# Down-projection steps between pairs of the up-projection, weight sums by accumulating loads, embedding projection moved

## Chip, core and metric

The kernel runs on one core of one Trainium2 chip. The metric is the device time of one launch in microseconds (us). The times shown are a median of three runs, and one further execution of the same program was profiled.

## What is computed

One decoder layer over 512 tokens of width 1024, in float32. The change lies in the last third, the gated MLP and the embedding behind it:

```python
h = rms_norm(x, ffn_norm[i])
act, lin = jnp.split(h @ w_ffn_up[i], 2, axis=-1)
act = causal_dwconv(act, w_ffn_conv[i]) + b_ffn_conv[i]
x = x + (jax.nn.gelu(act) * lin) @ w_ffn_down[i]
g = jax.nn.sigmoid(rms_norm(x, ple_norm[i]) @ w_ple_gate[i])
x = x + g * (p[i] @ w_ple_proj[i])
return rms_norm(x, final_norm)
```

The hidden width is 2816, 22 blocks of 128.

## The kernel before

Every float32 product is made of three matmuls on fp32r halves: a weight tile `raw` is loaded, ScalarE rounds it to `whi` (L164) and VectorE subtracts to get `wlo` (L165, the function `wsplit`); `raw` has four buffers in this part, `whi` and `wlo` four each, so a tile is split at most four split tiles ahead of its use. A step's weights are two split tiles, a pair's are four.

The up-projection goes in 11 pairs, `up(j)`: four products of 24 matmuls (two blocks of the gate half, two of the linear half), into the four PSUM banks of `mm_ps`. What follows each product (convolution, gelu, product of the halves) is done on ScalarE and VectorE; then `combine` (L277 to L286) makes from the pair's tile `g` the seven token-side factors of a Strassen-Winograd product, `ch` and `cl`. There is one buffer of these for four pairs.

The down-projection is three such products, `down(0)` to `down(2)`, over four, four and three pairs; `strassen` runs the seven steps. A step multiplies one factor by one block of the weights or by a sum of blocks, 24 matmuls (18 in down 2), and adds its result from PSUM to `x2` on VectorE (L1080). The blocks are loaded by SP, and the sums T1 to T4 are made in place by GpSimd or VectorE (L304). Down 0 runs after pair 4, down 1 after pair 10, down 2 straight behind it. In down 2, the additions are followed by the next norm (square on ScalarE, mean and power on GpSimd, L377 and L384; scaling on VectorE, L387), by the transposes x3n0T to x3n3T on TensorE (L410) and by copies to `h3h` and `h3l` (L412, L413).

Behind all that, p is loaded, transposed (pT, L1123) and multiplied by `w_ple_proj` (tiles pb from pTh); then comes the gate's product from `h3h`, and the end. A scheduler sets the order on each engine from the program order and from the priorities that `with ahead()` gives; each engine then works in that order.

Of the kernel before, what the change touches and what calls it, by code (L numbers as in the profile page):

```python
# [43 lines left out]
def tile_hybrid_block(  # L44
# [226 lines left out]

    WINO = ((0, "11"), (3, "T1"), (4, "T2"), (6, "22"), (1, "21"), (5, "T3"), (2, "T4"))

    def combine(g2, ch, cl, j):
# [3 lines left out]
        G.tensor_tensor(tmp[:, 0, :], a21, a22, op=ALU.add)  # L280
        G.tensor_tensor(tmp[:, 2, :], a1[:, 0, :], a21, op=ALU.subtract)
        G.tensor_tensor(tmp[:, 1, :], tmp[:, 0, :], a1[:, 0, :], op=ALU.subtract)
        G.tensor_tensor(tmp[:, 3, :], a1[:, 1, :], tmp[:, 1, :], op=ALU.subtract)
        for c, src in ((slice(0, 2), a1), (2, a22), (slice(3, 7), tmp)):
            S.copy(ch[:, c, j, :], src)
            V.tensor_tensor(cl[:, c, j, :], src, f32(ch[:, c, j, :]), op=ALU.subtract)  # L286

    def strassen(src, ch, cl, kh, add):
# [8 lines left out]
        pieces = [slice(k, min(k + 2, kh)) for k in range(0, kh, 2)]

        def sums(dst, x, y, eng):

            for q in pieces:
                eng.tensor_tensor(r[y][:, q, :], r[x][:, q, :], r[y][:, q, :], op=ALU.subtract)  # L304
# [4 lines left out]

        X = [mm_ps(f"sx{uid()}") for _ in range(2)]  # L310
        Z, Y = [], []
        for c, n in WINO:
            with ahead():
                if n == "11":
                    load(1, 1)
                    load(1, 2)
                    load(2, 2)
                elif n == "T1":
                    sums("T1", "12", "11", G)
                elif n == "T2":  # L320
                    sums("T2", "22", "T1", V)
                elif n == "21":
                    load(2, 1)
                elif n == "T3":

                    sums("T3", "22", "12", V)
                elif n == "T4":
                    sums("T4", "21", "T2", G)
                ws = split(n)
            if n == "T1":  # L330
                Z = [mm_ps(f"sz{uid()}") for _ in range(2)]
            elif n == "21":
                Y = [mm_ps(f"sy{uid()}") for _ in range(2)]
            ps = Z if n in ("T1", "22") else Y if n == "21" else X
            for t in range(2):
                tok = slice(t * P, (t + 1) * P)
                for k in range(kh):
                    hi, lo = ws[k // 2]
                    a, b = ch[:, c, k, tok], cl[:, c, k, tok]
                    first, last = k == 0 and n in ("11", "T1", "21"), k == kh - 1  # L340

                    TE.matmul(ps[t], lhsT=a, rhs=hi[:, k % 2, :], start=first, stop=False, skip_group_check=True)
                    TE.matmul(ps[t], lhsT=a, rhs=lo[:, k % 2, :], start=False, stop=False, skip_group_check=True)
                    TE.matmul(ps[t], lhsT=b, rhs=hi[:, k % 2, :], start=False, stop=last, skip_group_check=True)
                th, h = {"11": (0, 0), "T1": (2, 1), "T2": (0, 1), "22": (0, 1), "21": (0, 0), "T3": (2, 1), "T4": (2, 0)}[n]
# [769 lines left out]
    pt = [piece(f"pt{i}").rearrange("p (t d) -> p t d", t=2) for i in range(2)]  # L1115
    with ahead():
        for i in range(2):
            nc.sync.dma_start(pt[i], p[256 * i : 256 * i + 256, :].rearrange("(t q) d -> q t d", q=P))
    pT = []
    for k in range(2):  # L1120
        ps = sm_ps(f"pT{k}")
        for t in range(NT):
            TE.transpose(ps[:, t * P : (t + 1) * P], pt[t // 2][:, t % 2, k * P : (k + 1) * P], ident)  # L1123
        pT.append((piece(f"pTh{k}", R), piece(f"pTl{k}", R)))
        S.copy(pT[k][0], ps)
        V.tensor_tensor(pT[k][1], ps, f32(pT[k][0]), op=ALU.subtract)

    pj = [[piece(f"pj{t}_{h}") for h in range(2)] for t in range(NT)]
    for h in range(2):
        cols = slice(h * 512, (h + 1) * 512)  # L1130
        proj_b(w_ple_proj[:, cols], pT, 2, lambda t, ps: S.copy(pj[t][h], ps))
# [85 lines left out]
```

## Time and profile before

| | us |
|---|---|
| median of three runs | 1198.25 (1194.9 to 1203.29) |
| the profiled execution, its own time | 1203.02 |
| its span in the trace | 1201.2 |
| TensorE busy in it | 1164.5 |

The rows further down are of the profiled execution; its span starts at 0. PE is TensorE's matmul, DVE VectorE, ACT ScalarE, POOL GpSimd, SP the engine that issues most loads. A matmul's duration overlaps the next one's; the pace is the distance of two starts. Stretches in rows are in us from the start of the span.

### The profile page before, as it was taken

To read this page: it belongs to the slowest core of one execution; us is meant where nothing else is said; L and a number is where in the kernel's file an instruction comes from. 1 tells how busy PE (TensorE), PEld (TensorE's weight loads), DVE (VectorE), ACT (ScalarE), POOL (GpSimd) and SP (SyncE) were. 2 spreads that over 40 slices of the span, in tenths; PEclk is the share of its full clock that TensorE was granted. 3 is DMA by queue.
4 is the path that set the end of the run, shared out by engine and by line. 5 is a ranking of instruction groups with operands and counts; after the bars stand their busy time and mean duration, and the time that the engine had idled before them with its cause. 6 is when DMAs were issued, how large, how long until landed. Compare 5 with 4: busy or idle time off the path is not lost. (4 is left out here: it accounts for less than half of the span.)

```text
span 1201.2 us, 14024 instructions
## 1 busy us (share of the span) xinstructions
PE 1164.5 (97%) x5540; PEld 961.9 (80%) x5540; DVE 692.6 (58%) x810; ACT 515.5 (43%) x828; POOL 213.3 (18%) x213
## 2 busy tenths in 40 slices
PE   6999999999999999999999999999999999998796
PEld 6887787888887678888888888988888888876685
DVE  5866647667557546343333343566686665589735
ACT  4566283572382226443333232354334343343543
POOL 7003104031013000000110110112230211233202
PEclk9998999999999999999999999999999999999899
DMA  7332122222322243224233223633225333121501
GB/s 205 106 105 71 35 71 71 70 76 66 106 71 70 70 141 105 70 71 105 71 88 104 76 101 97 166 106 105 71 70 161 85 105 105 36 79 59 178 1 71
DMA packets 145825, 108.75 MB, mean 91 GB/s; under 512 B 5328, under 2 KB 124752, under 8 KB 145760
## 3 DMA queue, kind: packets, MB, share of 16 engines
q1 hardware_dynamic: 145184, 105.76, 30.2%
q10 hardware_dynamic: 576, 2.10, 0.5%
q8 instruction: 44, 0.72, 0.2%
q14 instruction: 21, 0.17, 0.0%
HBM read 105.75 MB, written 2.10 MB: 90 GB/s over the span
## 5 line engine op out<-in xcount | busy, mean ns | idle before, releaser
L165 DVE TENSOR_TENSOR wlo<-raw,whi 128x1024 fp32r<-128x1024 f32 x208 | 277.6, 1340 | 267.1 <-ACT whi L164 266.7
L164 ACT CAST whi<-raw 128x1024 fp32r<-128x1024 f32 (+2 forms) x209 | 216.5, 1039 | 388.4 <-PE pa L170 223.8
L169 PE MATMUL pa<-h1h,whi 128*128 128x512 f32 (+1 forms) x416 | 160.8, 387 | 0.2 <-ACT h1h L412 0.2
L171 PE MATMUL pa<-h1h,wlo 128*128 128x512 f32 (+1 forms) x416 | 157.9, 380 | 0.0
L170 PE MATMUL pa<-h1l,whi 128*128 128x512 f32 (+1 forms) x416 | 157.2, 378 | 0.1
L169 PE MATMUL pa<-h2h,whi 128*128 128x512 f32 (+1 forms) x384 | 142.8, 372 | 0.0
L170 PE MATMUL pa<-h2l,whi 128*128 128x512 f32 (+1 forms) x384 | 142.8, 372 | 0.0
L171 PE MATMUL pa<-h2h,wlo 128*128 128x512 f32 (+1 forms) x384 | 142.6, 372 | 0.0
L249 PE MATMUL pb<-whi,h1h 128*128 128x512 f32 x256 | 99.9, 395 | 0.8 <-DVE accb L677 0.8
L250 PE MATMUL pb<-wlo,h1h 128*128 128x512 f32 x256 | 99.9, 390 | 0.0
L251 PE MATMUL pb<-whi,h1l 128*128 128x512 f32 x256 | 99.5, 392 | 0.0
L169 PEld LDWEIGHTS pa<-h1h,whi 128*128 128x128 f32 x416 | 79.8, 192 | 15.2 <-issue 1.2
L170 PEld LDWEIGHTS pa<-h1l,whi 128*128 128x128 f32 x416 | 79.7, 192 | 14.7 <-issue 1.0
L171 PEld LDWEIGHTS pa<-h1h,wlo 128*128 128x128 f32 x416 | 79.5, 191 | 13.9 <-issue 0.2
L170 PEld LDWEIGHTS pa<-h2l,whi 128*128 128x128 f32 x384 | 72.4, 189 | 12.5
L169 PEld LDWEIGHTS pa<-h2h,whi 128*128 128x128 f32 x384 | 72.4, 188 | 12.4
L171 PEld LDWEIGHTS pa<-h2h,wlo 128*128 128x128 f32 x384 | 72.4, 189 | 12.4
L249 PEld LDWEIGHTS pb<-whi,h1h 128*128 128x128 f32 x256 | 48.1, 188 | 10.5 <-DVE accb L677 1.2
L251 PEld LDWEIGHTS pb<-whi,h1l 128*128 128x128 f32 x256 | 48.1, 188 | 9.8
L250 PEld LDWEIGHTS pb<-wlo,h1h 128*128 128x128 f32 x256 | 48.1, 188 | 9.3
L542 DVE SCALAR_TENSOR_TENSOR acc<-pa,prm,acc 128x511 f32<-128x511 f32 (+2 forms) x72 | 52.6, 742 | 2.9 <-ACT acc L540 2.0
L170 PE MATMUL pa<-obl,whi 128*128 128x512 f32 x128 | 52.0, 406 | 0.0
(375 smaller groups left out, 2036.7 us busy)
## 6 DMA issues: line engine op xcount, KB each, us to landing
raw<-in_w_in_dram SPq DMA_DIRECT2D x48, 512.0 KB, 5.2
raw<-in_w_ffn_up_dram SPq DMA_DIRECT2D x44, 512.0 KB, 5.1
raw<-in_w_in_dram SPq DMA_DIRECT2D x16, 1024.0 KB, 5.0
raw<-in_w_branch_b_dram SPq DMA_DIRECT2D x32, 256.0 KB, 3.7
raw<-in_w_ffn_down_dram SPq DMA_DIRECT2D x8, 1024.0 KB, 5.2
raw<-in_w_branch_a_dram SPq DMA_DIRECT2D x8, 512.0 KB, 4.8
raw<-in_w_out_dram SPq DMA_DIRECT2D x4, 1024.0 KB, 5.2
raw<-in_w_ple_gate_dram SPq DMA_DIRECT2D x4, 1024.0 KB, 5.2
```

Source lines behind the costliest of these rows:

```text
L164: S.copy(hi, raw)
L165: eng.tensor_tensor(lo, raw, f32(hi), op=ALU.subtract)
L169: TE.matmul(ps, lhsT=lh, rhs=rh, start=first, stop=False)
L170: TE.matmul(ps, lhsT=lh, rhs=rl, start=False, stop=False)
L171: TE.matmul(ps, lhsT=ll, rhs=rh, start=False, stop=last)
L249: TE.matmul(pss[t], lhsT=a, rhs=hi[:, kk, :], start=first, stop=False)
L250: TE.matmul(pss[t], lhsT=a, rhs=lo[:, kk, :], start=False, stop=False)
L251: TE.matmul(pss[t], lhsT=b, rhs=hi[:, kk, :], start=False, stop=last)
L542: V.scalar_tensor_tensor(out=acc[:, s:], in0=ps[:, : T - s], scalar=cw[:, ct, 3 - s : 4 - s], in1=acc[:, s:], op0=ALU.mult, op1=ALU.add,)
```

## The change

`strassen` becomes a generator that stops after each step; steps 0 to 2 of down 0 are laid behind pair 4, 3 to 5 behind pair 5 and step 6 behind pair 6; of down 1 behind pairs 8, 9 and 10. Down 2 runs its seven steps without a break. The signs of factors and sums are changed so that each sum of weight blocks is a plain sum, and each step loads its own tile: the first block by SP, every further one by an accumulating load that GpSimd issues (7 plain and 7 accumulating loads per down, up to three accumulating ones into one tile). The steps' PSUM banks come from the pool that the transposes use. `combine` computes on VectorE. p is loaded and transposed before down 2, into tiles of the g buffers, and the projected values are held in two raw tiles.

```diff
--- before.py
+++ after.py
-    WINO = ((0, "11"), (3, "T1"), (4, "T2"), (6, "22"), (1, "21"), (5, "T3"), (2, "T4"))
...
+    STEPS = (
+        (0, ("11",), "X", 0, 0, 1),
+        (3, ("11", "12"), "Z", 1, 1, -1),
+        (4, ("11", "12", "22"), "X", 0, 1, -1),
+        (6, ("22",), "Z", 0, 1, -1),
+        (1, ("21",), "Y", 0, 0, 1),
+        (5, ("12", "22"), "X", 1, 1, -1),
+        (2, ("11", "12", "21", "22"), "X", 1, 0, 1),
+    )
...
-        tmp = combine.pool.tile([P, 4, 256], F32, tag="cmb", name=f"cmb{uid()}", bufs=2)
-        G.tensor_tensor(tmp[:, 0, :], a21, a22, op=ALU.add)
-        G.tensor_tensor(tmp[:, 2, :], a1[:, 0, :], a21, op=ALU.subtract)
-        G.tensor_tensor(tmp[:, 1, :], tmp[:, 0, :], a1[:, 0, :], op=ALU.subtract)
-        G.tensor_tensor(tmp[:, 3, :], a1[:, 1, :], tmp[:, 1, :], op=ALU.subtract)
-        for c, src in ((slice(0, 2), a1), (2, a22), (slice(3, 7), tmp)):
+        t = pool.tile([P, 4, 256], F32, tag="cmb", name=f"cmb{uid()}", bufs=1)
+        V.tensor_tensor(t[:, 0, :], a22, a21, op=ALU.subtract)
+        V.tensor_tensor(t[:, 3, :], t[:, 0, :], a1[:, 0, :], op=ALU.add)
+        V.tensor_tensor(t[:, 1, :], a1[:, 0, :], a21, op=ALU.subtract)
+        V.tensor_tensor(t[:, 2, :], t[:, 3, :], a1[:, 1, :], op=ALU.subtract)
+        for c, src in ((slice(0, 2), a1), (2, a22), (3, t[:, 0, :]), (slice(5, 7), t[:, 1:3, :])):
             S.copy(ch[:, c, j, :], src)
             V.tensor_tensor(cl[:, c, j, :], src, f32(ch[:, c, j, :]), op=ALU.subtract)
+        S.activation(ch[:, 4, j, :], t[:, 3, :], AF.Copy, scale=-1.0)
+        V.scalar_tensor_tensor(
+            out=cl[:, 4, j, :], in0=t[:, 3, :], scalar=-1.0, in1=f32(ch[:, 4, j, :]),
+            op0=ALU.mult, op1=ALU.subtract,
+        )
...
-            for q in pieces:
-                eng.tensor_tensor(r[y][:, q, :], r[x][:, q, :], r[y][:, q, :], op=ALU.subtract)
...
-        X = [mm_ps(f"sx{uid()}") for _ in range(2)]
...
+        for n, (c, parts, b, th, h, sign) in enumerate(STEPS):
             with ahead():
+                raw = rp[0].tile([P, kh, 512], F32, tag="raw", name=f"raw{uid()}", bufs=rp[1])
+                for i, q in enumerate(parts):
+                    blk = v[int(q[0]) - 1][:, :, 512 * int(q[1]) - 512 : 512 * int(q[1])]
+                    if i == 0:
+                        nc.sync.dma_start(raw, blk)
+                    else:
+                        nc.gpsimd.dma_start(raw, blk, accum_op=ALU.add)
+                ws = [wsplit(raw[:, k : min(k + 2, kh), :], min(2, kh - k), 512) for k in range(0, kh, 2)]
+            new = b not in banks
+            if new:
+                banks[b] = [sm_ps(f"s{b}{uid()}") for _ in range(2)]
...
+                    add(2 * th + t, h, ps, sign, n)
+            yield
...
-                acts[n0] = cmp.tile([P, 2, T], F32, tag="g2", name=f"g2_{n0}", bufs=4)
+                acts[n0] = cmp.tile([P, 2, T], F32, tag="g2", name=f"g2_{n0}", bufs=5)
...
-    for j in range(5):
+    def over(q):
+        done[0] = q + 1
+        with ahead(50000):
+            for j in sorted(acts):
+                if j // 8 == q + 1:
+                    comb(j // 2)
+
+    for j in range(4):
         up(j)
-    down(0)
-    with ahead(50000):
-        comb(4)
-    for j in range(5, 11):
+    d = down(0)
+    for j, n in ((4, 3), (5, 3), (6, 1)):
         up(j)
+        run(d, n)
+    over(0)
+    up(7)
     g3 = gain_bc(lnp, "g3", ple_norm)
-    down(1)
-    with ahead(50000):
-        for j in range(8, 11):
-            comb(j)
+    d = down(1)
+    for j, n in ((8, 3), (9, 3), (10, 1)):
+        up(j)
+        run(d, n)
+    over(1)
     h3 = new_hT("h3")
-    down(2)
-    fax.close()
...
+    pt = quad("pt").rearrange("p a (t d) -> p (a t) d", t=2)
+    nc.sync.dma_start(pt, p.rearrange("(t q) d -> q t d", q=P))
+    pTh, pTl = quad("pTh", R), quad("pTl", R)
...
+    run(down(2), 7)
+    pjs = [rp[0].tile([P, 4, 512], F32, tag="raw", name=f"pj{i}", bufs=rp[1]) for i in range(2)]
...
+    fax.close()
```

Two functions of the new part read:

```python
    def run(d, n):
        for _ in range(n):
            next(d)

    def quad(name, dt=F32):
        return cmp.tile([P, 2, T], dt, tag="g2", name=name, bufs=5)
```

The first place is GpSimd's order at the end of down 2, before: the sums (L304) that end in the tile of T4 (raw468), and the norm of the first two token blocks.

```order
L304 TENSOR_TENSOR raw468_7889<-raw469_7891,raw468_7889 128x1024
L304 TENSOR_TENSOR raw468_7889<-raw469_7891,raw468_7889 128x512
L304 TENSOR_TENSOR raw468_7889<-raw481_8025,raw468_7889 128x1024
L304 TENSOR_TENSOR raw468_7889<-raw481_8025,raw468_7889 128x512
L377 TENSOR_SCALAR x3n0s_8005<-x3n0s_8005 128x1
L377 TENSOR_SCALAR x3n1s_8021<-x3n1s_8021 128x1
```

And now: accumulating loads of steps 1, 2, 5 and 6 of down 2 (raw477, raw482, raw493, raw496).

```order
L321 DMA raw466_7855<-in_w_ffn_down_dram 128x4x512 x3
L321 DMA raw477_7991<-in_w_ffn_down_dram 128x3x512
L321 DMA raw482_8024<-in_w_ffn_down_dram 128x3x512 x2
L321 DMA raw493_8168<-in_w_ffn_down_dram 128x3x512
L321 DMA raw496_8211<-in_w_ffn_down_dram 128x3x512 x2
L368 TENSOR_SCALAR x3n0s_8078<-x3n0s_8078 128x1
L368 TENSOR_SCALAR x3n1s_8094<-x3n1s_8094 128x1
L368 TENSOR_SCALAR x3n0s_8078<-x3n0s_8078 128x1
L375 TENSOR_TENSOR x3n0r_8079<-x3n0s_8078,neghalf_78 128x1
L321 DMA raw496_8211<-in_w_ffn_down_dram 128x3x512
```

The sums have left the engine's order; loads stand in it, and the third one of step 6 behind the power x3n0r.

The second place is VectorE's order at steps 1 and 2 of down 2, before: sums of weights (L304), splits (L165) and the additions to x (L1080).

```order
L304 TENSOR_TENSOR raw469_7891<-raw470_7893,raw469_7891 128x512
L165 TENSOR_TENSOR wlo474_7930<-raw468_7889,whi474_7929 128x512
L1080 TENSOR_TENSOR x2_0_5307<-x2_0_5307,sx466_7887 128x512
L1080 TENSOR_TENSOR x2_1_5308<-x2_1_5308,sx467_7888 128x512
L304 TENSOR_TENSOR raw468_7889<-raw470_7893,raw468_7889 128x1024
L304 TENSOR_TENSOR raw468_7889<-raw470_7893,raw468_7889 128x512
```

And now; raw482 is step 2's tile, whose buffer step 6's tile takes.

```order
L1124 TENSOR_TENSOR pTl_7944<-pT0_7945,pTh_7943 128x512
L1124 TENSOR_TENSOR pTl_7944<-pT1_7952,pTh_7943 128x512
L1070 TENSOR_TENSOR x2_0_5307<-x2_0_5307,sX475_7969 128x512
L1070 TENSOR_TENSOR x2_1_5308<-x2_1_5308,sX476_7970 128x512
L165 TENSOR_TENSOR wlo483_8029<-raw482_8024,whi483_8028 128x1024
L165 TENSOR_TENSOR wlo484_8033<-raw482_8024,whi484_8032 128x512
```

The sums are gone from between the splits; the split that frees raw482 stands behind step 0's additions.

The third place is TensorE's order at the third token block's transposes, before: the end of step 6 (sx467), then the transposes, then p.

```order
L344 MATMUL sx467_7888<-whi489_8143,cl_5682 128x512
L410 MATMUL x3n2T0_8161<-ident_73,x3n2_0_8115 128x128 x4
L410 MATMUL x3n2T1_8169<-ident_73,x3n2_1_8116 128x128 x4
L410 MATMUL x3n3T0_8190<-ident_73,x3n3_0_8131 128x128 x4
L410 MATMUL x3n3T1_8198<-ident_73,x3n3_1_8132 128x128 x4
L1123 MATMUL pT0_8213<-ident_73,pt0_8209 128x128 x2
```

And now: the embedding projection's first half (pb502) stands ahead of x3n2T, its second half (pb505 to pb508) behind.

```order
L249 MATMUL pb502_8287<-whi504_8290,pTh_7943 128x512
L250 MATMUL pb502_8287<-wlo504_8291,pTh_7943 128x512
L251 MATMUL pb502_8287<-whi504_8290,pTl_7944 128x512
L401 MATMUL x3n2T0_8238<-ident_73,x3n2_0_8189 128x128 x4
L401 MATMUL x3n2T1_8246<-ident_73,x3n2_1_8190 128x128 x4
L401 MATMUL x3n3T0_8267<-ident_73,x3n3_0_8205 128x128 x4
L249 MATMUL pb505_8322<-whi510_8328,pTh_7943 128x512
```

The matmuls of the first half have moved from behind the transposes to between step 6 and x3n2T.

## Rows read from the trace of the kernel before

**Rows 1.** The page: busy us (share of the span) and instructions by engine.

```profile
PE 1164.5 (97%) x5540; PEld 961.9 (80%) x5540; DVE 692.6 (58%) x810; ACT 515.5 (43%) x828; POOL 213.3 (18%) x213
```

**Rows 2.** Stretches: PE, PEld, DVE, ACT, POOL busy (x); PEclk, DMA share, GB/s.

```profile
1040.00:1060.00 20.00, 20.00 (x90) 16.59 (x89) 16.38 (x15) 5.81 (x6) 4.81 (x2) 1.00 0.00 1
1060.00:1080.00 20.00, 18.92 (x82) 14.96 (x81) 15.55 (x18) 10.93 (x13) 5.59 (x4) 1.00 0.38 118
1080.00:1100.00 20.00, 16.73 (x63) 12.44 (x62) 18.98 (x23) 7.23 (x11) 4.65 (x3) 0.91 0.13 40
1120.00:1140.00 20.00, 13.80 (x66) 11.55 (x65) 15.62 (x22) 8.87 (x19) 5.39 (x6) 0.83 0.56 203
```

**Rows 3.** TensorE's waits, whole span: us in total, times, longest.

```profile
PE x3n2T L410 <- DVE x3n L387: 5.9, 1, 5.9
PE sz L343 <- DVE wlo L165: 1.8, 1, 1.8
```

**Rows 4.** Timeline of TensorE: start us, us, instruction, [idle before, releaser].

```profile
756.25 1.04 PE L410 MATMUL x2n0T<-ident,x2n 128*128 128x128 f32 x8
757.04 0.48 PE L249 MATMUL pb<-whi,mth 128*128 128x512 f32 x1
...
1044.90 0.39 PE L342 MATMUL sx<-whi,ch 128*128 128x512 f32 x1
...
1050.34 0.39 PE L342 MATMUL sz<-whi,ch 128*128 128x512 f32 x1
...
1093.26 0.63 PE L343 MATMUL sz<-wlo,ch 128*128 128x512 f32 x1
1093.68 0.63 PE L344 MATMUL sz<-whi,cl 128*128 128x512 f32 x1
...
1124.36 0.39 PE L344 MATMUL sx<-whi,cl 128*128 128x512 f32 x1
1130.62 1.94 PE L410 MATMUL x3n2T<-ident,x3n 128*128 128x128 f32 x8 [5.88 <-DVE x3n L387]
...
1134.02 1.04 PE L1123 MATMUL pT<-ident,pt 128*128 128x128 f32 x8
...
1135.35 0.50 PE L249 MATMUL pb<-whi,pTh 128*128 128x512 f32 x1 [0.29 <-ACT pTh L1125]
```

**Rows 5.** Groups of instructions, 735 to 1141 us: busy us, mean ns | idle before.

```profile
L165 DVE TENSOR_TENSOR wlo<-raw,whi 128x1024 fp32r<-128x1024 f32 x92 | 129.8, 1419 | 48.1 <-ACT whi L164 47.9
...
L304 DVE TENSOR_TENSOR raw<-raw,raw 128x1024 f32<-128x1024 f32 (+1 forms) x12 | 14.3, 1203 | 4.4 <-POOL raw L304 4.3
...
L304 POOL TENSOR_TENSOR raw<-raw,raw 128x1024 f32<-128x1024 f32 (+1 forms) x12 | 28.8, 2406 | 45.4 <-DVE wlo L165 45.4
...
L164 ACT CAST whi<-raw 128x1024 fp32r<-128x1024 f32 x92 | 93.2, 1019 | 131.4 <-PE pa L170 75.1 <-PE sx L344 19.3 <-PE sz L344 16.1
```

**Rows 6.** Timeline of GpSimd and VectorE in down 2.

```profile
1083.24 3.31 POOL L304 TENSOR_TENSOR raw<-raw,raw 128x1024 f32<-128x1024 f32 x1 [3.56 <-DVE wlo L165]
1084.22 2.88 DVE L165 TENSOR_TENSOR wlo<-raw,whi 128x512 fp32r<-128x512 f32 x1
...
1087.03 0.68 DVE L1080 TENSOR_TENSOR x<-x,sx 128x512 f32<-128x512 f32 x1
...
1087.62 1.80 DVE L286 TENSOR_TENSOR cl<-g,ch 128x256 fp32r<-128x256 f32 x3
...
1091.09 1.21 DVE L165 TENSOR_TENSOR wlo<-raw,whi 128x1024 fp32r<-128x1024 f32 x1
...
1092.82 0.68 DVE L165 TENSOR_TENSOR wlo<-raw,whi 128x512 fp32r<-128x512 f32 x1
```

**Rows 7.** Loads by tile: KB each, median us from issue to landing.

```profile
raw<-in_w_ffn_down_dram SPq DMA_DIRECT2D x8, 1024.0 KB, 5.2
...
raw<-in_w_ffn_down_dram SPq DMA_DIRECT2D x4, 768.0 KB, 4.7
...
raw<-in_w_ple_proj_dram SPq DMA_DIRECT2D x2, 512.0 KB, 3.6
```

More of the change, by code (lines that the diff above doesn't have):

```diff
@@ new lines, in combine @@
+    def combine(pool, g2, ch, cl, j):
+        t = pool.tile([P, 4, 256], F32, tag="cmb", name=f"cmb{uid()}", bufs=1)
+        a1, a21, a22 = g2[:, :, :256], g2[:, 0, 256:], g2[:, 1, 256:]
+        V.tensor_tensor(t[:, 0, :], a22, a21, op=ALU.subtract)
[3 more added lines that the diff above has]
+        for c, src in ((slice(0, 2), a1), (2, a22), (3, t[:, 0, :]), (slice(5, 7), t[:, 1:3, :])):
@@ L299, in strassen @@
-        pieces = [slice(k, min(k + 2, kh)) for k in range(0, kh, 2)]
-        def sums(dst, x, y, eng):
-            for q in pieces:
-                eng.tensor_tensor(r[y][:, q, :], r[x][:, q, :], r[y][:, q, :], op=ALU.subtract)
-            r[dst] = r.pop(y)
-        def split(n):
-            return [wsplit(r[n][:, q, :], q.stop - q.start, 512) for q in pieces]
-        X = [mm_ps(f"sx{uid()}") for _ in range(2)]
-        Z, Y = [], []
-        for c, n in WINO:
-            with ahead():
[L314 to L334, printed above, removed]
@@ new lines, in strassen @@
+        banks = {}
+        for n, (c, parts, b, th, h, sign) in enumerate(STEPS):
+            with ahead():
+                raw = rp[0].tile([P, kh, 512], F32, tag="raw", name=f"raw{uid()}", bufs=rp[1])
[9 more added lines that the diff above has]
+                banks[b] = [sm_ps(f"s{b}{uid()}") for _ in range(2)]
@@ L335, in strassen @@
             for t in range(2):
+                ps = banks[b][t]
                 tok = slice(t * P, (t + 1) * P)
@@ L338, in strassen @@
                     hi, lo = ws[k // 2]
[L339 to L345, printed above, removed]
+                    a_h, a_l = ch[:, c, k, tok], cl[:, c, k, tok]
+                    TE.matmul(ps, lhsT=a_h, rhs=hi[:, k % 2, :], start=new and k == 0, stop=False, skip_group_check=True)
+                    TE.matmul(ps, lhsT=a_h, rhs=lo[:, k % 2, :], start=False, stop=False, skip_group_check=True)
+                    TE.matmul(ps, lhsT=a_l, rhs=hi[:, k % 2, :], start=False, stop=k == kh - 1, skip_group_check=True)
                 with ahead(50000):
-                    add(th + t, h, ps[t], n)
+                    add(2 * th + t, h, ps, sign, n)
+            yield
     def rsqrt_mean(dst, ssq, inv, n):
@@ L1036, in tile_hybrid_block @@
     cl = cmp.tile([P, 7, 4, 256], R, name="cl")
-    combine.pool = cmp
     acts, done = {}, [0]
     def comb(j):
-        combine(acts[2 * j], ch, cl, j % 4)
+        combine(cmp, acts[2 * j], ch, cl, j % 4)
     def up_emit_for(n0):
@@ L1076, in down, with add @@
         last = 4 * q + kh == KF // 2
-        def add(t, h, ps, n):
+        def add(t, h, ps, sign, n):
             xs = x2[t][:, h * 512 : (h + 1) * 512]
-            V.tensor_tensor(xs, xs, ps, op=ALU.add)
+            V.tensor_tensor(xs, xs, ps, op=ALU.add if sign > 0 else ALU.subtract)
             if not last:
                 return
-            if (t < 2 and n == "22") or n == "T3":
+            if n in (3, 5):
                 nms[t] = Norm(lnp, x2[t], f"x3n{t}")
@@ L1087, in add @@
                 nms[t].gather()
-            elif n in ("21", "T4"):
+            elif n in (4, 6):
                 nms[t].square(0)
                 norm_T(nms[t], g3, h3, t)
-        strassen(w_ffn_down[1024 * q : 1024 * q + 256 * kh, :], ch, cl, kh, add)
-        done[0] = q + 1
-    for j in range(5):
+        return strassen(w_ffn_down[1024 * q : 1024 * q + 256 * kh, :], ch, cl, kh, add)
+    def run(d, n):
+        for _ in range(n):
+            next(d)
+    def over(q):
+        done[0] = q + 1
+        with ahead(50000):
[3 more added lines that the diff above has]
+    for j in range(4):
         up(j)
-    down(0)
-    with ahead(50000):
-        comb(4)
-    for j in range(5, 11):
+    d = down(0)
+    for j, n in ((4, 3), (5, 3), (6, 1)):
         up(j)
+        run(d, n)
+    over(0)
+    up(7)
     g3 = gain_bc(lnp, "g3", ple_norm)
-    down(1)
-    with ahead(50000):
-        for j in range(8, 11):
-            comb(j)
-    h3 = new_hT("h3")
-    down(2)
+    d = down(1)
[3 more added lines that the diff above has]
+    over(1)
+    h3 = new_hT("h3")
+    def quad(name, dt=F32):
[3 more added lines that the diff above has]
+    pTh, pTl = quad("pTh", R), quad("pTl", R)
+    for k in range(2):
+        ps = sm_ps(f"pT{k}")
+        for t in range(NT):
+            TE.transpose(ps[:, t * P : (t + 1) * P], pt[:, t, k * P : (k + 1) * P], ident)
+        S.copy(pTh[:, k, :], ps)
+        V.tensor_tensor(pTl[:, k, :], ps, f32(pTh[:, k, :]), op=ALU.subtract)
+    run(down(2), 7)
+    pjs = [rp[0].tile([P, 4, 512], F32, tag="raw", name=f"pj{i}", bufs=rp[1]) for i in range(2)]
+    pj = [[pjs[t // 2][:, 2 * (t % 2) + h, :] for h in range(2)] for t in range(NT)]
+    for h in range(2):
+        cols = slice(h * 512, (h + 1) * 512)
+        proj_b(w_ple_proj[:, cols], (pTh, pTl), 2, lambda t, ps: S.copy(pj[t][h], ps))
     fax.close()
@@ L1113, in piece @@
         return gtp.tile([P, T], dt, tag="g", name=name, bufs=24)
[L1115 to L1131, printed above, removed]
     g4 = gain_bc(lnp, "g4", final_norm)
```

6 lines of the change are left out of this document (removed).

## Prediction

> **What bounds the kernel now.** I read the page first. TensorE is busy 97% of the span, VectorE 58%, GpSimd 18% [rows 1]. So a change of the order can earn only what TensorE waits, and the question is where that is. The table of stretches then shows it: from 1040 to 1060 us TensorE is busy for all of 20 us with 90 matmuls; the stretches that start at 1060, 1080 and 1120 us have 82, 63 and 66, while VectorE is busy 15.6 to 19.0 us of 20, and in the last two the granted clock is 0.91 and 0.83 [rows 2]. This is the end of the second product (down 1) and all of the third (down 2). The list of what TensorE waited for over the whole span shows what the waits are: 5.9 us once for x3n2T, and several of under 2 us in the steps, the longest 1.8 us for a split of weights [rows 3]; for the steps the same list of 1040 to 1142 us alone has the same sums. Down 0, before it, therefore waits for nothing today.
>
> The timeline of TensorE gives the price [rows 4]. Steps 0 and 1 of down 1 start at 1044.90 and 1050.34 us: 24 matmuls in 5.44 us, 0.2267 us each. Eight transposes take 757.04 - 756.25 = 0.79 us at full clock. From 1044.90 to 1135.35 us (the first matmul of the embedding projection) are 90.45 us. In them lie 7 x 24 + 7 x 18 = 294 matmuls (66.65 us) and 40 transposes (3.95 us). So 19.85 us are lost. The last matmul of down 2 starts at 1124.36, so it is over at 1124.59: 10.76 us from there to 1135.35, less 24 transposes (2.37), are 8.4 us lost in the norm after the last step (the wait of 5.9 us for x3n2T, then transposes at half pace); the other 11.5 us are lost between about 1077 us and 1124 us, where weight sums, combines, splits and the additions to x all stand on VectorE. These 19.9 us, 1.7% of the time, are all that the change can win.
>
> **The change part by part.**
>
> *Steps between pairs.* In down 0 and in steps 0 to 5 of down 1 there is no wait to hide, so laying them between pairs earns nothing there. The last step (the sum of four blocks) of both comes after a pair, and down 2 still runs its seven steps in a row. What the interleaving gives is time for the loads of downs 0 and 1.
>
> *Weight sums.* Twelve VectorE sums (14.3 us) and twelve GpSimd sums (28.8 us) go [rows 5]. The four 128x256 operations of each combine go from GpSimd to VectorE; at 0.6 us for such a piece [rows 6] they are 2.4 us, 26 us for the eleven, over 400 us. Against this, a split of 128x512 that takes 0.68 us alone took 2.88 us beside a GpSimd sum [rows 6], and the 92 splits, 85 of 128x1024 (1.21 us alone) and 7 of 128x512, take 129.8 us [rows 5] where 107.6 would do: 22 us of VectorE time that come free with the sums. Nothing of this is on TensorE's path in downs 0 and 1, where VectorE idles 48 us before splits [rows 5].
>
> *What the sums cost now.* Every step loads its own raw tile: one plain load from SP and 0 to 3 accumulating loads from GpSimd, each waiting for the one before. Per down 7 plain and 7 accumulating loads stand where 4 plain ones stood, on SP ahead of the next pair's loads and on GpSimd ahead of whatever it computes next. The trace has no accumulating load, so I bound it. From below it is a plain load: 4.7 us for 768 KB, 5.2 for 1 MB [rows 7]. From above I take three plain loads in a row (fetch, read what is there, write): 14.1 and 15.6 us. The value I take: 512 KB in the same 2 KB rows land in 3.6 us, 1 MB in 5.2, so 2.0 us are fixed and 3.2 us go with each MB; the accumulating load must move source and destination, so its moving part counts twice: **A = 2.0 + 2 x 3.2 = 8.4 us for 1 MB, a = 2.0 + 2 x 2.4 = 6.8 us for 768 KB**, nearer to the row below than to the bound above. A busy queue makes this longer: 38.5 MB instead of 11 cross it. In 103 us of three pairs and seven steps that is 21 MB with the double count; by 203 GB/s at a share of 0.56 [rows 2] these need about 60 us of the engines, and the pairs another 23. Not full, but not idle.
>
> The rule of the Trainium skill that bears on it (Collectives: The Full Stack, The bandwidth ceiling) is that an add inside the DMA is not slow by its arithmetic but because it needs two source reads. With the fixed 2.0 us and 436 GB/s of DMA: Bandwidth & Descriptors (Anatomy of one DMA) an estimate by these pages is 2.0 + 2 x 1.8 = 5.6 us for 768 KB, and the sum below would come to about 1190 us. No run here shows such a load; the plain loads of this trace are slower than that formula gives, so I stay with the rows.
>
> *Step 6 of downs 0 and 1* (three accumulating loads). Its raw tile takes the place of step 4's, which is split at the end of the pair before (four split tiles ahead). From there TensorE has steps 3 to 5 and a pair: (72 + 96) x 0.2267 = 38.1 us. The chain is 3.0 (the casts and splits that free the tile) + 5.2 + 3A + 2.3 (a cast of 1.0 [rows 5], a split of 1.21 [rows 6]) = 10.5 + 3A = 35.7 us: just in time; late from A = 9.2 us on. ScalarE has the cast of these weights in front of the pair's gelu, so it would stand still from a smaller A on, but the pair has four banks to write into. Cost: 0, with 2.4 us of cover.
>
> *Step 6 of down 2* has no such cover. Its tile becomes free when step 2's weights are split. VectorE's order (the second place shown above) puts the two additions of step 0 ahead of that, and behind step 6 of down 1 combine pieces, splits and pT: from that step's end on eight pieces of 0.68 us, two of 1.21 and three of 0.6 [rows 6], 9.7 us, against 4.9 us of TensorE work (pT and step 0): free 4.8 us after the end of step 0. Then 4.7 + 3a + 2.3, so the weights are there 11.8 + 3a after it. TensorE has steps 1 to 5 (90 matmuls, 20.4 us), eight transposes (0.8) and the waits of the next paragraph (1.0): 22.2 us. **The wait is 3a - 10.4 = 10.0 us.** GpSimd's third load stands behind the power of x3n0 (first place); that comes before the second load has landed, so it adds nothing at a = 6.8. The steps' banks now come from the pool of the transposes, which makes the second Y bank wait for x3n0T's copies, some 3.7 us; that lies inside the 10.0.
>
> *Start of down 2.* The same VectorE queue of 9.7 us against 9.0 us of TensorE work until step 2: 1.0 us.
>
> *Embedding projection.* Today it runs behind all transposes (third place); now 20 of its matmuls (4.5 us) and eight transposes (0.8) lie between step 6 and x3n2T. The wait of 5.9 us falls, but VectorE splits the late weights before it gets to x3n1 and x3n2: 2.0 us left. p loads early into a free g tile; its transposes cost what they cost before. Holding the projected values in two raw tiles leaves two for the gate's weights; their splits need split tiles in any case, 0.
>
> *Clock.* After the waits of today the clock is at the lower of its two levels, 1.2 instead of 2.4 GHz: matmuls start 0.42 us apart from 1093.26 us on (seven of them, 1.4 us lost), and the 16 transposes from 1130.62 to 1134.02 us take 3.4 us instead of 1.6 [rows 4]. After a wait of 10 us the same is due: 2.5 us.
>
> **Sum.** Lost after: 1.0 + 10.0 + 2.0 + 2.5 = 15.5 us, against 19.9: 4.4 us gained. The profiled execution took 1203.0 us (span 1201.2), so 1198.6; it is 4.8 us above the median of the runs shown, 1198.25, and from the median the same gain gives **1194 us**.
>
> **The rivals.**
> 1. *The accumulating load is as cheap as a plain one* (a = 4.7). For it: the DMA engines' share is 0.00 to 0.56 in these stretches [rows 2], so it would find them free. Then step 6 waits 3 x 4.7 - 10.4 = 3.7 us, the clock loses 1.0, the sum of losses is 7.7: 12.2 us gained, **1186 us**.
> 2. *The accumulating load is dear* (the other side). One mechanism: the chain of three loads in a row that each wait for the last. Decisive from a = 7.6 us (A = 9.4) on, where 3a - 10.4 + 5.5 and twice a 0.6 us of lateness in downs 0 and 1 use up the 19.9. At a = 10, A = 12: 19.6 in down 2, 10.5 + 36 - 38.1 = 8.4 in each of downs 0 and 1, 5.5 for the rest, 41.9 in all: 22 us slower, **1220 us**. For it: the DMA engines are about 80% busy by the estimate above, and GpSimd has to issue every one of these loads in order. Against it: 768 KB of plain load land only 0.5 us sooner than 1 MB [rows 7], so moving bytes is not the larger part. With the bound from above (14.1, 15.6) it would be 31.9 + 2 x 19.2 + 5.5 - 19.9, 56 us slower.
> 3. *The change hides nothing*: down 2 stays bound by VectorE as today, step 6 is late by a little, and the projection only changes places with a wait: **1198 us**. For it: VectorE has 3.3 us of work (two additions of 0.68, splits of 1.21 and 0.68) for each 4.1 us step of down 2 even without sums. Against it: without them it has 0.8 us to spare in each.
>
> The Trainium skill (SBUF — State Buffer, SBUF: two separate sides) has a rule that speaks for the second: loads issued from GpSimd stand still while VectorE holds a port that both share, since GpSimd cannot write their descriptors. No run here shows it.
>
> **How the numbers follow.** Forecast (a between about 5.3 and 8.9) 0.43; rival 1 0.25; rival 2 0.22; rival 3 0.10. Over 1% (12 us, about what a measurement of this kernel can tell from no change) faster needs rival 1: 0.25. Over 1% slower is rival 2 from a = 9 on (16.6 + 5.5 + 2 x 5.7 - 19.9 = 13.6): 0.22. The rest, 0.53, is within 1%. The range goes from a little under rival 1, 1183 us, to rival 2, 1222 us; the upper bound of the load's price is left out.
>
> **What would show it.** Right: the accumulating loads land in 6 to 8 us; in down 2 TensorE waits about 10 us for step 6's weights, the only long wait; no wait in downs 0 and 1; x3n2T waits under 3 us. Wrong: a landing time near 5 us (rival 1) or above 8 us with TensorE waiting before the last step of downs 0 and 1 (rival 2); or VectorE full and many waits of 1 to 2 us through down 2 (rival 3). The forecast falls if step 6's tile is loaded much earlier than when step 2 is split, or if downs 0 and 1 lose time where they lose none now.

## The result and the profile after

The change makes the kernel about 1% slower: 1210.3 us (median of 13 runs, 1207.7 to 1218.6) against 1201.3 us for the kernel before in the same comparison (13 runs, 1194.9 to 1205.2), ratio 1.010 (1.007 to 1.013). 1194 us were forecast; 1210 lies in the stated range, on the side of rival 2.

The profiled execution took 1207.67 us, its span is 1205.9. A span is not compared with a span here, because the unchanged part in front ran at a different clock in the two profiles (granted clock of the first 250 us 0.97 before, 1.00 after): x2n0T starts at 756.25 us before [rows 4] and at 750.01 us after. From there to the end it is 1201.2 - 756.25 = 445.0 us before and 1205.9 - 750.01 = 455.9 us after, 10.9 us more. All stretches below are counted this way, "the last part" for short.

The page of the kernel after (busy us and share; a DMA queue with packets, MB and share of 16 engines; groups; loads with KB each and us to landing):

```profile
PE 1161.5 (96%) x5540; PEld 958.6 (79%) x5540; DVE 665.8 (55%) x864; ACT 518.7 (43%) x850; POOL 160.6 (13%) x178
...
q0 software_dynamic: 10192, 20.19, 9.7%
...
L321 POOL DMA_DIRECT2D raw<-in_w_ffn_down_dram x21 | 27.2, 1373 | 330.0 <-DVE wlo L165 184.6
...
raw<-in_w_ffn_down_dram SPq DMA_DIRECT2D x14, 1024.0 KB, 5.3
raw<-in_w_ffn_down_dram POOLq DMA_DIRECT2D x14, 1024.0 KB, 10.4
...
raw<-in_w_ffn_down_dram SPq DMA_DIRECT2D x7, 768.0 KB, 5.2
raw<-in_w_ffn_down_dram POOLq DMA_DIRECT2D x7, 768.0 KB, 8.5
```

VectorE and GpSimd are relieved as the diff promises (692.6 and 213.3 us before [rows 1], 665.8 and 160.6 now). TensorE waited for VectorE before [rows 3], so this was worth something; how much, only the last experiment below shows, since here a new and longer wait has come. The line to see is the landing time of the loads that GpSimd issues: 10.4 us where 8.4 were assumed, 8.5 where 6.8 were. Each also keeps GpSimd busy for 1.4 us (L321).

What TensorE waited for after (us in total, times, longest), against [rows 3]:

```profile
PE sX L333 <- ACT whi L164: 12.6, 4, 6.1
...
PE x3n0T L401 <- DVE x3n L378: 1.3, 1, 1.3
...
PE x3n2T L401 <- DVE x3n L378: 0.9, 1, 0.9
```

The wait for x3n2T has shrunk from 5.9 to 0.9 us as intended, and 12.6 us before steps of the X bank have come. The releaser named is ScalarE, which rounds the weights. The next views show that ScalarE itself was waiting for the load. TensorE at the places where it stops, after:

```profile
750.01 1.03 PE L401 MATMUL x2n0T<-ident,x2n 128*128 128x128 f32 x8
...
945.70 0.39 PE L171 MATMUL pa<-h2h,wlo 128*128 128x512 f32 x1
947.58 0.50 PE L333 MATMUL sX<-whi,ch 128*128 128x512 f32 x1 [1.50 <-ACT whi L164]
948.84 0.80 PE L334 MATMUL sX<-wlo,ch 128*128 128x512 f32 x1 [0.76 <-DVE wlo L165]
...
1075.04 0.39 PE L171 MATMUL pa<-h2h,wlo 128*128 128x512 f32 x1
1078.83 0.80 PE L333 MATMUL sX<-whi,ch 128*128 128x512 f32 x1 [3.40 <-ACT whi L164]
1080.09 0.80 PE L334 MATMUL sX<-wlo,ch 128*128 128x512 f32 x1 [0.46 <-DVE wlo L165]
...
1081.11 0.63 PE L333 MATMUL sX<-whi,ch 128*128 128x512 f32 x1
...
1108.60 0.73 PE L333 MATMUL sX<-whi,ch 128*128 128x512 f32 x2 [1.53 <-ACT whi L164]
...
1116.34 1.32 PE L401 MATMUL x3n0T<-ident,x3n 128*128 128x128 f32 x8 [1.33 <-DVE x3n L378]
1118.80 0.56 PE L333 MATMUL sY<-whi,ch 128*128 128x512 f32 x1 [1.14 <-DVE h3l L404]
...
1128.86 1.22 PE L333 MATMUL sX<-whi,ch 128*128 128x512 f32 x2 [6.14 <-ACT whi L164]
```

The starts at 947.58, 1078.83 and 1128.86 us are step 6 of downs 0, 1 and 2. After each, starts are 0.43 us apart instead of 0.23 for a while. (The start at 1108.60 us is step 5 of down 2, for whose weights TensorE waits 1.53 us.) GpSimd's issues of step 6's three accumulating loads, down by down, say why:

```profile
916.22 1.28 POOL L321 DMA_DIRECT2D raw<-in_w_ffn_down_dram  x1 [25.38 <-DVE wlo L165]
927.44 1.28 POOL L321 DMA_DIRECT2D raw<-in_w_ffn_down_dram  x1 [9.95 <-DMA raw<-in_w_ffn_down_dram]
937.03 1.28 POOL L321 DMA_DIRECT2D raw<-in_w_ffn_down_dram  x1 [8.31 <-DMA raw<-in_w_ffn_down_dram]
...
1045.61 1.28 POOL L321 DMA_DIRECT2D raw<-in_w_ffn_down_dram  x1 [25.44 <-DVE wlo L165]
1056.71 1.28 POOL L321 DMA_DIRECT2D raw<-in_w_ffn_down_dram  x1 [9.82 <-DMA raw<-in_w_ffn_down_dram]
1069.16 3.88 POOL L321 DMA_DIRECT2D raw<-in_w_ffn_down_dram  x3 [11.16 <-DMA raw<-in_w_ffn_down_dram]
...
1103.31 1.26 POOL L321 DMA_DIRECT2D raw<-in_w_ffn_down_dram  x1 [3.18 <-DVE x L1070]
1112.68 1.27 POOL L321 DMA_DIRECT2D raw<-in_w_ffn_down_dram  x1 [8.11 <-DMA raw<-in_w_ffn_down_dram]
...
1120.33 1.32 POOL L321 DMA_DIRECT2D raw<-in_w_ffn_down_dram  x1 [4.83 <-DMA raw<-in_w_ffn_down_dram]
```

The second and third of each wait for the landing of the one before ("<-DMA raw"; the row of 1069.16 us holds the first loads of two steps of down 2 as well). The chain ends with the first rounding of the summed weights, on ScalarE, for the three downs:

```profile
946.48 1.99 ACT L164 CAST whi<-raw 128x1024 fp32r<-128x1024 f32 x2 [13.61 <-DMA raw<-in_w_ffn_down_dram]
...
1077.73 1.04 ACT L164 CAST whi<-raw 128x1024 fp32r<-128x1024 f32 x1 [17.80 <-DMA raw<-in_w_ffn_down_dram]
...
1127.76 2.51 ACT L164 CAST whi<-raw 128x1024 fp32r<-128x1024 f32 x3 [9.48 <-DMA raw<-in_w_ffn_down_dram]
```

From the first issue to this point: 946.48 - 916.22 = 30.3 us, 1077.73 - 1045.61 = 32.1 us, 1127.76 - 1103.31 = 24.5 us, or 10.1, 10.7 and 8.2 us a load.

The single loads are not alike: from issue to the next one, or to the rounding, they are 11.2, 9.6 and 9.5 us in down 0, 11.1, 12.5 and 8.6 us in down 1, and 9.4, 7.7 and 7.4 us for the smaller ones of down 2. The stretches from issue to landing of four of them (columns as in [rows 2]) show what goes with it:

```profile
1045.61:1056.43 10.82, 10.82 (x49) 8.98 (x48) 8.78 (x15) 6.81 (x10) 1.28 (x1) 1.00 0.87 173
1056.71:1068.87 12.16, 12.16 (x55) 10.10 (x54) 4.00 (x6) 0.78 (x1) 1.28 (x1) 1.00 0.97 254
1069.16:1077.65 8.49, 6.27 (x28) 4.87 (x26) 0.00 (x0) 0.00 (x0) 3.88 (x3) 1.00 0.82 142
1120.33:1127.68 7.35, 2.39 (x6) 1.33 (x5) 0.00 (x0) 0.00 (x0) 1.32 (x1) 0.73 0.69 107
```

The last load is alone: its 768 KB (0.79 MB) in 7.35 us are the 107 GB/s. The 1 MB (1.05 MB) of the first two are 97 and 86 GB/s, and the rest of the 173 and 254 GB/s belongs to other loads, of pairs and of the next steps. With little beside it, a load that adds lands in 8.5 us (1 MB) or 7.4 us (768 KB).

Stretches after, the first three beside [rows 2] (PE, PEld, DVE, ACT, POOL busy; granted clock, DMA share, GB/s):

```profile
1040.00:1060.00 20.00, 20.00 (x90) 16.58 (x89) 15.31 (x23) 9.70 (x13) 2.56 (x2) 1.00 0.80 204
1060.00:1080.00 20.00, 16.23 (x70) 12.72 (x68) 2.65 (x3) 2.27 (x3) 3.88 (x3) 0.95 0.90 183
1080.00:1100.00 20.00, 18.57 (x73) 14.60 (x74) 18.72 (x32) 11.47 (x20) 2.42 (x2) 0.88 0.85 211
...
1078.80:1086.00 7.20, 6.71 (x17) 4.96 (x18) 6.25 (x8) 4.21 (x6) 0.30 (x1) 0.57 1.10 243
```

Where the DMA engines had a share of 0.00 to 0.38 they now have 0.80 to 0.90. The work of a stretch is not the same as before: from 1060 to 1080 us it is now mostly a pair of the up-projection. VectorE is busy only 2.65 us of 20 there, because ScalarE, which comes ahead of it, stands 17.80 us before the rounding shown above. The kernel has gone from waiting for VectorE to waiting for loads.

### The profile page after: what moved, and what is told of

It is laid out like the page before. It is cut to its first block, busy times and chain, and to the rows that moved or that the text cites. A ratio compares the mean times of both kernels' runs of the same rounds, so it can differ in the third digit from the quotient of the medians.

```text
span 1205.9 us, 14072 instructions
## 1 busy us (share of the span) xinstructions
PE 1161.5 (96%) x5540; PEld 958.6 (79%) x5540; DVE 665.8 (55%) x864; ACT 518.7 (43%) x850; POOL 160.6 (13%) x178
## 3 DMA queue, kind: packets, MB, share of 16 engines
q0 software_dynamic: 10192, 20.19, 9.7%
## 4 chain that ended last, share of the span: by engine, by line
PE 84%; DMA 6%; DVE 4%; issue 2%; ACT 2%; POOL 1%; SPq 1%; POOLq 0%; ACTq 0%; DVEq 0%
PE pa L170 16%; PE pa L169 16%; PE pa L171 16%; PE pb L249 7%; PE pb L251 7%; PE pb L250 7%; DMA raw<-in_w_ffn_down_dram 5%; PE yd L608 2%; PE sX L333 1%; PE sX L334 1%; PE sX L335 1%; PE st L616 1%; DVE wlo L165 1%; PE yo L605 1%; DMA raw<-in_w_in_dram 1%
## 5 line engine op out<-in xcount | busy, mean ns | idle before, releaser
L165 DVE TENSOR_TENSOR wlo<-raw,whi 128x1024 fp32r<-128x1024 f32 x208 | 255.6, 1234 | 305.3 <-ACT whi L164 305.0
L171 PEld LDWEIGHTS pa<-h2h,wlo 128*128 128x128 f32 x384 | 72.4, 188 | 12.5
L169 PEld LDWEIGHTS pa<-h2h,whi 128*128 128x128 f32 x384 | 72.3, 188 | 12.5
L321 POOL DMA_DIRECT2D raw<-in_w_ffn_down_dram x21 | 27.2, 1373 | 330.0 <-DVE wlo L165 184.6
L249 PEld LDWEIGHTS pb<-whi,h1h 128*128 128x128 f32 x256 | 48.1, 188 | 10.5 <-DVE accb L668 1.2
## 6 DMA issues: line engine op xcount, KB each, us to landing
raw<-in_w_ffn_down_dram POOLq DMA_DIRECT2D x14, 1024.0 KB, 10.4
```

Of the source, the lines that this page charges most:

```text
L169: TE.matmul(ps, lhsT=lh, rhs=rh, start=first, stop=False)
L171: TE.matmul(ps, lhsT=ll, rhs=rh, start=False, stop=last)
L249: TE.matmul(pss[t], lhsT=a, rhs=hi[:, kk, :], start=first, stop=False)
L321: nc.gpsimd.dma_start(raw, blk, accum_op=ALU.add)
```

## The experiments

Before each, the text on record; in it, theory A is the chain of loads, and the rivals are named there.

**First blocks alone.**

```diff
-                        nc.gpsimd.dma_start(raw, blk, accum_op=ALU.add)
+                        continue
```

> This kernel is the changed one with all 21 accumulating loads left out, so every step multiplies by the first block of its sum alone. Theory A (chain): what the change lost is the row of up to three accumulating loads, 8.1 us a link in down 2 and 9.6 us in downs 0 and 1; without them no step waits for weights, downs 0 and 1 lose nothing and down 2 loses only its start and the norm, some 7 us; from the first x2n0T transpose to the end of the span about 432 us (455.9 in the changed kernel, 445.0 before), time about 1188 us. Theory B (VectorE and PSUM): the loss comes from the combines on VectorE and from the steps' banks shared with the transposes; then it stays above 445 us for that stretch, above 1198 us.

Measured, with the added blocks left out of every sum: 1183.2 us, ratio to before 0.986 (0.981 to 0.991); last part 1181.3 - 750.16 = 431.1 us. In downs 0 to 2 TensorE waits nowhere over 0.6 us, and 2.8 us for x3n2T. With the same order, the same work on VectorE and the same banks, 24.8 of the 455.9 us go when the accumulating loads go. So the loads are the loss, by their chain, their traffic or their place on GpSimd, and neither VectorE nor the banks stand behind it.

**The chain with plain loads.**

```diff
-                        nc.gpsimd.dma_start(raw, blk, accum_op=ALU.add)
+                        nc.gpsimd.dma_start(raw, blk)
```

> The accumulating loads are replaced by plain loads of the same blocks into the same tile from the same queue, one after the other; so the tile holds the last block and not the sum. It tells what the adding costs against the mere chain. Theory A with the price in the adding (a second stream of reads): each link falls from 8.1 to about 6 us in down 2 and from 9.6 to about 6.6 us, the waits before step 6 of downs 0 and 1 go (10.5 + 20 us against 38.1), in down 2 it falls from 6.1 us to under 1; the stretch from x2n0T to the end about 436 us, time about 1192 us. Theory A with the price in the issue from GpSimd and its fixed latency: the links stay above 7.5 us, time above 1200 us.

Measured: 1186.8 us, ratio 0.989 (0.984 to 0.994); last part 434.7 us, so 21.2 of the 24.8 us go with the adding alone. One wait for step 6's weights is left, 2.3 us in down 2, where under 1 was expected. Its page (queue, issues, landing):

```profile
q0 software_dynamic: 5264, 20.19, 5.0%
...
L321 POOL DMA_DIRECT2D raw<-in_w_ffn_down_dram x21 | 16.0, 764 | 320.3 <-DMA raw<-in_w_ffn_down_dram 172.3
...
raw<-in_w_ffn_down_dram POOLq DMA_DIRECT2D x14, 1024.0 KB, 7.3
...
raw<-in_w_ffn_down_dram POOLq DMA_DIRECT2D x7, 768.0 KB, 5.4
```

The same 21 loads and 20.19 MB in the same queue and order. What the adding costs: 3.1 us of the median landing for either size (10.4 against 7.3, 8.5 against 5.4), almost twice the packets (10192 against 5264), twice the time of the DMA engines (9.7% against 5.0%), and 1373 instead of 764 ns of GpSimd an issue. The median of 7.3 us, against 5.3 for SP's loads of 1 MB in the same run, is not the price of GpSimd's queue, since it mixes loads with and without company. Two of 1 MB, from issue to landing:

```profile
845.23:850.89 5.66, 5.66 (x27) 4.68 (x26) 2.57 (x5) 2.19 (x4) 0.76 (x1) 1.00 0.60 185
851.18:860.15 8.97, 8.97 (x42) 7.41 (x41) 5.12 (x10) 4.37 (x7) 0.75 (x1) 1.00 0.75 236
```

The first is alone (1.05 MB in 5.66 us are the 185 GB/s), the second moves half of the 236 GB/s. Alone against alone, the adding costs 8.5 - 5.7 = 2.8 us for 1 MB, and GpSimd's queue (5.7 against SP's 5.3 us) about half a microsecond.

**Two half chains a tile.**

```diff
-                        nc.gpsimd.dma_start(raw, blk, accum_op=ALU.add)
+                        for s in (slice(0, 2), slice(2, kh)):
+                            nc.gpsimd.dma_start(raw[:, s, :], blk[:, s, :], accum_op=ALU.add)
```

(The plain loads are cut in the same way.)

> Each load of a step's tile is cut in two along the blocks of rows, so that two chains of half the size run side by side (42 accumulating loads instead of 21, the same bytes). Theory A, latency: a link of half the size takes some 6.5 us, both chains run at once, three links 20 us instead of 24 to 29: the waits before step 6 of downs 0 and 1 (3.4 and 1.5 us by the list of waits) go and the one in down 2 falls from 6.1 to about 2 us; about 1201 us. Theory C (volume): the DMA engines, busy 80 to 86 percent there, set the pace; then the chains take as long as before and GpSimd's 1.3 us per issue come on top; 1210 to 1215 us.

Measured: 1201.2 us, ratio to before 1.001 (0.998 to 1.004), last part 447.2 us: 9 us faster than the change, and no better than before. A half lands in 8.3 us for 512 KB, beside its twin, so half the bytes take off a fifth. Downs 0 and 1 have no wait left over 0.7 us, as expected of the shorter chains. The 1201 us on record came out by luck: down 2 has no wait of 2 us before step 6, but one of 2.7 us for a factor at its start and a new one of 8.0 us for x3n0T. GpSimd's timeline there:

```profile
1104.64 2.19 POOL L323 DMA_DIRECT2D raw<-in_w_ffn_down_dram  x2 [7.22 <-DMA raw<-in_w_ffn_down_dram]
1106.91 0.18 POOL L370 TENSOR_SCALAR x3n0s<-x3n0s 128x1 f32<-128x1 f32 x1
...
1110.58 1.24 POOL L323 DMA_DIRECT2D raw<-in_w_ffn_down_dram  x1 [3.21 <-DMA raw<-in_w_ffn_down_dram]
1112.01 0.89 POOL L323 DMA_DIRECT2D raw<-in_w_ffn_down_dram  x1 [0.20 <-issue]
1112.63 0.58 POOL L370 TENSOR_SCALAR x3n0s<-x3n0s 128x1 f32<-128x1 f32 x1
1113.31 0.56 POOL L377 TENSOR_TENSOR x3n0r<-x3n0s,neghalf 128x1 f32<-128x1 f32 x1
```

The norm's last two small operations stand behind the third pair of issues, which wait for the second pair's landing. An accumulating load that waits holds up everything behind it on GpSimd: here the norm by about 5.5 us, from 1107.1 us (the end of its operation at 1106.91) to 1112.63.

**The embedding part alone.** The kernel before, with p's transposes ahead of down 2 and the projection's input and output in tiles that do not wait for down 2's to be freed:

```diff
-    down(2)
-    fax.close()
...
+    pt = quad("pt").rearrange("p a (t d) -> p (a t) d", t=2)
+    nc.sync.dma_start(pt, p.rearrange("(t q) d -> q t d", q=P))
...
+    down(2)
...
+    pjs = [rp[0].tile([P, 4, 512], F32, tag="raw", name=f"pj{i}", bufs=rp[1]) for i in range(2)]
```

> The kernel before with only the third part of the change: p loaded and transposed ahead of down 2 and the embedding projection's first half between step 6 and x3n2T. The prediction's term: the wait of 5.9 us falls to about 2, the transposes run at full clock (1.8 us): 5 to 6 us faster, 1195 to 1196 us where the kernel before is at 1201. Rival: VectorE is the bound in down 2 and the projection's splits and copies come into its and ScalarE's queues; no gain, 1200 to 1202 us.

Measured: 1192.3 us, a little under the 1195 to 1196 expected, ratio 0.994 (0.991 to 0.997); last part 1188.5 - 749.88 = 438.6 us, 6.3 less than before. The wait for x3n2T is gone; the steps' waits stay (the longest 3.0 us, for a split). So the third part of the change earns 6 us, and the other two together cost about 10.9 + 6.3 = 17 us, if the parts add up.

**Step 2's sum kept for step 6.** Step 6 needs 11+12+21+22, and step 2's tile holds 11+12+22 already:

```diff
-                raw = rp[0].tile([P, kh, 512], F32, tag="raw", name=f"raw{uid()}", bufs=rp[1])
+                if n == 6:
+                    raw, parts = kept[0], ("21",)
+                else:
+                    raw = rp[0].tile([P, kh, 512], F32, tag="raw", name=f"raw{uid()}", bufs=rp[1])
+                if n == 2:
+                    kept.append(raw)
...
-    for j, n in ((4, 3), (5, 3), (6, 1)):
+    for j, n in ((4, 2), (5, 5), (6, 0)):
```

(Likewise for pairs 8 to 10; `over` is called right behind step 6.)

> The changed kernel, with the tile of step 2 (blocks 11+12+22) kept and step 6's sum made in it by one accumulating load of block 21, in place of a fresh load and three accumulating ones: 11 loads a down instead of 14, 5 of them accumulating instead of 7, about 8.3 MB less moved. Four steps must then follow one another, so the order is changed too: two steps after pair 4 (8), five after pair 5 (9), none after pair 6 (10), and the coefficient sums of the next down are begun right behind step 6. Theory A (the chain of three accumulating loads before step 6 is the loss): step 6 has steps 3 to 5 (3 x 5.4 us, in down 2 3 x 4.1 us) for one landing of 10.4 us (8.5 us), so no wait is left in downs 0 and 1 and at most 3 us in down 2: 1183 to 1188 us, about as the kernel with first blocks alone. Rival C (GpSimd's queue as a whole: any accumulating load that blocks it holds up the norms and the next load): 5 of 7 accumulating loads are still there, so down 2 keeps some 8 us of waits and the time is 1192 to 1200 us.

**The same order without keeping the sum.** Only the second hunk of the diff above.

> The changed kernel with the order of the kernel that keeps step 2's sum (two steps after pair 4 or 8, five after pair 5 or 9, none after pair 6 or 10, coefficient sums begun right behind step 6), but with step 6's own tile loaded and three times added to as in the change. Theory A: the tile for step 6 now comes free at the split of step 2 and has three steps, about 16 us and what the split is ahead, for a chain of 5.3 + 3 x 10 = 35 us, instead of two steps and a pair of the up-projection (5.4 + 5.4 + 21.8 = 33 us): some 15 to 20 us of wait before step 6 in each of downs 0 and 1 where the change has 4 and 7, so 1225 to 1240 us. Rival D (the place of the pairs does not matter, only the count of adding loads): 1210 us as the change.

Measured together: 1187.3 us, ratio 0.989 (0.986 to 0.992), last part 434.7 us, against 1233.8 us, ratio 1.028 (1.024 to 1.032), last part 481.2 us. Both as theory A has it. TensorE's waits in the second:

```profile
PE pa L169 <- ACT whi L164: 31.4, 4, 16.4
PE x3n0T L401 <- DVE x3n L378: 11.4, 1, 11.4
```

Two waits of 14.5 and 16.4 us make up the first line. They stand before a pair's first matmul and not before step 6, since ScalarE rounds in order and step 6's late weights are in front of the pair's. In the first kernel the longest wait of downs 0 to 2 is 0.7 us, although five of seven accumulating loads a down are still there, and land no sooner (9.0 us for 1 MB and 10.0 us for 768 KB in the median). So neither their number nor their place in GpSimd's queue costs by itself (rival C out), but three in a row in front of one step. And the room for the chain decides: with one pair less in front of it, in two downs, the last part is 481.2 - 455.9 = 25.3 us longer than in the change. (Down 2, whose order is the same in both, loses about as much as in the change, 19.0 us against 19.7 by the distances of starts, though its wait now stands before x3n0T.)

**The kept sum, in one piece.** The same, with (4, 7) and (8, 7): seven steps without a pair between, as in the kernel before.

> The kernel that keeps step 2's sum, with all seven steps of downs 0 and 1 in one piece behind pair 4 and pair 8, as in the kernel before (pairs 5, 6 and 9, 10 follow; the coefficient sums of the next down are begun behind them as far as their pairs are done). Theory A (the interleaving matters only because it sets how long an adding chain has; with chains of one and two landings nothing is left to hide): no wait over 2 us in downs 0 and 1, and within 5 us of the interleaved one, 1184 to 1192 us. Rival D2 (the interleaving itself pays, by spreading 11 loads of a down over more time, since the DMA engines are busy to 0.8 and more): waits of some 8 us in each of downs 0 and 1, 1200 to 1206 us.

Measured: 1186.3 us, ratio 0.989 (0.986 to 0.992); last part 1183.0 - 751.72 = 431.3 us, next to the 431.1 us of the kernel that has no accumulating loads. The waits of the last part over 0.5 us are two:

```profile
PE x3n2T L407 <- DVE x3n L384: 2.8, 1, 2.8
PE sX L340 <- DVE wlo L165: 0.6, 1, 0.6
```

The interleaving itself earns nothing (rival D2 out). Both versions that keep the sum beat the kernel before and the changed one, and by 5 and 6 us of the median the embedding part alone (their ratios to before just touch its own). From that part's 438.6 us to 431.3 us are 7.3 us, one profile each: that is what the rest of the change, with its relief of VectorE and GpSimd, is worth once no long row of loads stands in the way.

## Why the prediction was wrong

TensorE's loss, taken as the prediction took it (each distance of two starts over the pace at full clock), is 20.5 us of the last part before and 30.9 us after: 10.4 of the 10.9 us above, and the other half a microsecond lies behind the last matmul. By the prediction's steps:

| step | predicted us | in the trace after |
|---|---|---|
| step 6 of down 0, late by | 0 | 2.7 |
| step 6 of down 1, late by | 0 | 4.6 |
| start of down 2 | 1.0 | 1.7 |
| waits inside down 2 | 10.0 | 10.1 |
| around x3n2T | 2.0 | 2.5 |
| lower clock after waits (after: the rest) | 2.5 | 9.3 |
| sum | 15.5 | 30.9 |

*Step 6 of downs 0 and 1* is the step that failed, by the size of A: the term for the traffic beside the load was named and then put at nothing. Its model of the step was right: with the measured 30.3 and 32.1 us for 3A, 10.5 + 3A - 38.1 gives 2.7 and 4.5 us, and the gaps before the first matmuls at 947.58 and 948.84 us are 1.65 + 1.03 us over the pace, those at 1078.83 and 1080.09 us 3.56 + 1.03. A was put at 8.4 us and is 10.1 to 10.7 in the mean, past the 9.2 at which the prediction said lateness begins. The price of such a load by itself came out: 8.5 us with little beside it (8.4 forecast) and 7.4 for 768 KB (6.8 forecast), of which the adding is 2.8 us for 1 MB (3.2 forecast for the second MB). "A busy queue makes this longer" and "not full, but not idle" stand in the prediction, but no term follows from them, and with other loads beside them five of the six links took 9.5 to 12.5 us. That this is the traffic's doing is read from the stretches of two traces; no run changed the traffic alone. (The estimate of it has a slip: the 6.3 MB of three pairs need 17 us at its rate, not 23, so a share of 0.75 and not 0.8; measured are 0.80 to 0.90. The 5.6 us for 768 KB that the prediction estimated by the Trainium skill (DMA: Bandwidth & Descriptors, Anatomy of one DMA) is further off the measured 7.4 and 8.5. Whether a port that VectorE holds, of which the Trainium skill speaks (SBUF — State Buffer, SBUF: two separate sides), has a part in the longer landings, no run here tells.)

*The clock* is the other term that failed. One stop was reckoned with; there are three before step 6 and two around 1117 us, and after them TensorE runs at the lower of its two levels for a while: 0.57 in the mean from 1078.8 to 1086 us, so 1.2 instead of 2.4 GHz for most of it, after 3.8 us without the start of a matmul. What the starts lose beyond the gaps is 1.5 us in down 0, 2.5 in down 1 and 5.3 in down 2, nearly half as much as the waits themselves.

*Down 2*: the sum of the waits came out (1.53 + 1.33 + 1.14 + 6.14 us), but not as the one wait that was described. It stands in four places, and a chain of 24.5 us instead of 3 x 6.8 = 20.4 was partly hidden by the others: step 6 was late by less because TensorE had been late already.

*Weight sums*: the relief of VectorE that was reckoned with is on the page. In downs 0 and 1 it was off the path, as said; in down 2 the chain of loads took its place, and with the sum kept it shows in the 7.3 us above. *Steps between pairs* earn nothing by themselves, as said; the kernel with the sum kept and all steps in one piece shows it.

*Embedding projection* was right: 2.5 us left where 2.0 were forecast, and alone it gives 6.3 us.

*Rival 2* was what happened, with its own sign on record: landing above 8 us and TensorE waiting before the last step of downs 0 and 1. With 30.3, 32.1 and 24.5 us for the chains its sum is 2.7 + 4.5 + (24.5 - 10.4) + 5.5 - 19.9 = 6.9 us slower; the clock adds 6.8 to that, and the partly hidden chain of down 2 takes 4.0 off, which leaves 9.7 of the 10.4. (By its own sum the rival is decisive a little above a = 7.6, where it uses up 19.1 of the 19.9 us.) The likeliness of it was put too low: what spoke for it, engines about 80% busy, was on record without a price, and no row of the trace had an adding load.

## What to carry to other kernels

Price a load that adds by its landing in a chain and in the traffic that it will meet, not by its bytes: here three in a row took 24 to 32 us, so the first question is how many of them stand in front of one consumer and what work lies beside them. A partial sum that an earlier step has left in its tile was worth more here than room for a longer chain: one added block in place of a fresh load and three added ones turned 1210 us into 1186. And when a relieved engine brings nothing, look for what the relief put on a queue that works in order.

## What was not expected of the hardware

- Adding in the load cost about twice the packets and twice the engine time of the same bytes (10192 against 5264 packets, 9.7% against 5.0%), and 1373 against 764 ns of GpSimd an issue. The Trainium skill (Collectives: The Full Stack, The bandwidth ceiling) says of the add in a reduce-scatter that it is slow by its second source read; the engine time here agrees.
- Landing depends more on what else is moved than expected: adding loads of 1 MB took from 8.5 us with little beside them to 12.2 us in one trace, plain ones of the same queue 5.7 to 9.0 us in the two stretches shown. Cutting a load in two that run side by side brought 10.4 us down to 8.3 only. The chain was left on GpSimd's queue in all runs: by the Trainium skill (DMA: Bandwidth & Descriptors, SWDGE vs HWDGE vs iDMA) accumulating is a feature of the loads that GpSimd issues, and no run here tried another.
